# A hybrid decoder layer in fp32: transposed rows kept as two halves in DRAM, one root for four tiles of q and k, and the engine of low halves and sums set by stage

## The chip, the cores and the metric

The kernel runs on one core of a Trainium2 chip. The metric is the device time of one execution in microseconds, and a kernel is judged by the median of several executions. Engines are named as the profile names them: PE does matrix products (PEld loads their weights), DVE is the vector engine, ACT the scalar engine, POOL is GpSimd, and SP issues all DMA transfers. Each engine works through its own list of instructions strictly in order.

## The reference, cut to what matters

One decoder layer on 2048 tokens of width 1024. A projection feeds two groups of heads, a short convolution and a dilated attention; their outputs are projected back, and a gated feed-forward layer and a gated embedding follow.

```python
h = rmsnorm(x, g_mix);  zb, zc, zx, zq, zk, zv = split(h @ w_in)          # 6 x 512 columns
y_c = zb * causal_dwconv3(zc * zx, conv_w, conv_b)
q = rmsnorm(zq by head of 64, q_norm_g);  k = rmsnorm(zk by head of 64, k_norm_g)
y_a = dilated_attention(q, k, zv)          # three causal windows, ALiBi, merged by denominators
x = x + concat(rmsnorm(y_c, g_out_conv), rmsnorm(y_a, g_out_attn)) @ w_out
h = rmsnorm(x, g_ffn)
x = x + (silu(causal_dwconv3(h @ w_gate)) * (h @ w_up)) @ w_down           # d_ff = 2816
x = x + sigmoid(rmsnorm(x, g_ple) @ w_ple_gate) * (p @ w_ple_proj)
```

## The kernel before, in words

**Products.** Every fp32 operand is split into a high half (`split`: a cast on ACT) and a low half (source minus high half, L94, on DVE or POOL), and `mm3` (L97) sums three products: high by high, high by low, low by high. Transposes go through PE (L124, L198, L799).

**Stages.** By the trace: `qkv` runs from 0 to about 345 us, `mix` (attention, with the convolution's products woven in) to about 980, then `rest`: `project` to about 1200, `gate_up(0)` to 1660, `down(0)` to 1875, `gate_up(1)` to 2310, `down(1)` to 2530, `ple` to the end. Four blocks c of 512 tokens, each of four tiles j of 128, are worked through in `qkv`.

**qkv.** `head` normalizes a tile of x (root on one column, L75 to L84, then `hn`, L115), transposes it and splits it into `hT` (halves, L126 and L127). POOL then adds the two halves again (L173, 128x1024) into a staging tile `raw` and SP stores that fp32 sum to `hd[c]`. The staging tiles are three, and `load_w` loads the weights through the same three. `project` multiplies, and `normed` (L187 to L190) takes a tile of q or k in PSUM: squares on ACT, sums per head and a root of 8 columns on DVE, then the scaled tile `qn` or `kn`, read from PSUM. A root is 12 small instructions (`rsqrt`: three of set-up, then three rounds of three). `spill` transposes q or k once all four tiles are there and stores them to `qd` or `kd`, from where the attention loads `qs` and `kk`.

**The convolution's rows.** `load_conv_h(c)` loads `hd[c]` again, eight tiles of 128x512, and splits each into `hq`: a cast on ACT, a subtraction on POOL. It runs for c = 0 before the attention begins, and once for each further c in the midst of it.

**rest.** `stream` loads weights and splits them into operands `w`, up to four ahead of the products. The engine of the low half is `shared()`: a turn through three, of which one goes to POOL and two to DVE. `shared()` also places the sums of squares in `project` (`square`, L830) and a sum in `down` (L1048). A generator in the background prepares the other operand of the next stage (`right`): seven low halves for each quarter, of which those of indices 4 and 6 are named DVE and those of 5 and 3 POOL. `products` and `left` are one level of Strassen's scheme, hence seven products where there were eight. `reciprocal_root` makes a column of sums by PE (L836), copies it to SBUF (L838), takes a root on DVE (12 small instructions, L840 at its end), and the four evacuations of the product (L902) wait for it. `sums_of_w_down` makes, during `gate_up(0)`, four differences of each pair of rows of w_down (L959, 128x512, DVE) for the later stage.

**The order.** A scheduler places the instructions on each engine when the program is built; the source order is a preference and no guarantee.

## Time and profile before

| what | value |
|---|---|
| median of 3 executions | 2756.98 us (2752.61 to 2761.0) |
| the profiled execution, its own time | 2758.95 us |
| its span, first to last instruction | 2757.2 us |
| mean granted TensorE clock | 0.983 |
| busy: PE, DVE, ACT, POOL | 2621.5, 2006.8, 1321.2, 784.3 us |

Busy time of an engine counts an instruction from its start to its end, including time in which it was held up inside. Time idle before an instruction is put down to what released it. The clock of PE has two levels, 1.2 and 2.4 GHz, and the profile gives the granted share of the higher one.

### The profile page before, as it was taken

To read this page: it belongs to the slowest core of one execution; us is meant where nothing else is said; L and a number is where in the kernel's file an instruction comes from. 1 tells how busy PE (TensorE), PEld (TensorE's weight loads), DVE (VectorE), ACT (ScalarE), POOL (GpSimd) and SP (SyncE) were. 2 spreads that over 40 slices of the span, in tenths; PEclk is the share of its full clock that TensorE was granted. 3 is DMA by queue.
4 is the path that set the end of the run, shared out by engine and by line. 5 is a ranking of instruction groups with operands and counts; after the bars stand their busy time and mean duration, and the time that the engine had idled before them with its cause. 6 is when DMAs were issued, how large, how long until landed. Compare 5 with 4: busy or idle time off the path is not lost. (4 is left out here: it accounts for less than half of the span.)

```text
span 2757.2 us, 37506 instructions
## 1 busy us (share of the span) xinstructions
PE 2621.5 (95%) x12320; PEld 2169.0 (79%) x12320; DVE 2006.8 (73%) x3878; ACT 1321.2 (48%) x2941; POOL 784.3 (28%) x527
## 2 busy tenths in 40 slices
PE   7999989999999989899999999989999999998999
PEld 5777878888888778777788888767888887877887
DVE  8766656867677665998888778567888877557655
ACT  3332357877777344454344345444444435444332
POOL 5111311524343621123222223122222223223332
PEclk9999989999999999999999999999999999999999
DMA  5544565665756688568633346663323336666332
GB/s 191 153 138 123 169 163 139 184 184 146 205 154 180 220 279 296 196 228 274 241 114 105 107 142 227 216 233 115 102 101 107 104 111 218 220 217 204 103 130 85
DMA packets 283860, 470.04 MB, mean 170 GB/s; under 512 B 32656, under 2 KB 101904, under 8 KB 283664
## 3 DMA queue, kind: packets, MB, share of 16 engines
q1 hardware_dynamic: 283664, 467.64, 53.4%
q8 instruction: 97, 1.59, 0.2%
q14 instruction: 99, 0.81, 0.1%
HBM read 339.53 MB, written 127.99 MB: 170 GB/s over the span
## 5 line engine op out<-in xcount | busy, mean ns | idle before, releaser
L97 PE MATMUL ps<-t,w 128*128 128x512 f32 x4368 | 1024.3, 395 | 16.1 <-DVE w L94 9.5
L97 PEld LDWEIGHTS ps<-t,w 128*128 128x128 f32 x4368 | 819.6, 188 | 207.7 <-DVE w L94 12.4
L97 PE MATMUL ps<-w,g 128*128 128x512 f32 x1368 | 339.0, 397 | 26.9 <-DVE t L902 6.2
L97 PEld LDWEIGHTS ps<-w,g 128*128 128x128 f32 x1368 | 257.3, 190 | 89.0 <-DVE t L902 7.3
L94 POOL TENSOR_TENSOR w<-raw,w 128x512 fp32r<-128x512 f32 x100 | 144.9, 1449 | 564.1 <-ACT w L93 364.0
L97 PE MATMUL zps<-hq,chi 128*128 128x512 f32 x768 | 256.8, 411 | 5.3 <-DVE yc L327 5.3
L93 ACT CAST w<-raw 128x512 fp32r<-128x512 f32 x318 | 193.7, 616 | 119.5 <-PE ps L97 111.7
L289 POOL TENSOR_TENSOR clo<-craw,chi 128x512 fp32r<-128x512 f32 x96 | 126.4, 1322 | 389.8 <-ACT chi L288 144.2
L93 ACT CAST w<-s 128x512 fp32r<-128x512 f32 x208 | 128.3, 619 | 224.7 <-PE ps L97 200.5
L97 PE MATMUL ps<-w,t 128*128 128x512 f32 x852 | 211.6, 394 | 9.1 <-DVE w L94 5.9
L94 POOL TENSOR_TENSOR w<-s,w 128x512 fp32r<-128x512 f32 x70 | 111.8, 1597 | 368.7 <-ACT w L93 300.0
L438 ACT ACTIVATE pt<-so,md 128x256 f32<-128x256 f32 (+1 forms) x384 | 175.1, 458 | 79.9 <-DVE md L435 78.0
L97 PEld LDWEIGHTS ps<-w,t 128*128 128x128 f32 x852 | 159.0, 188 | 49.5 <-DVE w L94 8.8
L94 DVE TENSOR_TENSOR w<-raw,w 128x512 fp32r<-128x512 f32 x218 | 177.1, 816 | 15.5 <-ACT w L93 15.5
L435 DVE CUSTOM_DVE_ANT_0 so<-s,neg 128x256 f32<-128x256 f32 (+1 forms) x384 | 130.4, 362 | 60.9 <-PE s L432 47.3
L97 PEld LDWEIGHTS zps<-hq,chi 128*128 128x128 f32 x768 | 142.3, 195 | 29.6 <-DVE yc L327 6.1
L97 PE MATMUL zps<-hq,clo 128*128 128x512 f32 x384 | 154.3, 402 | 0.0
L432 PE MATMUL s<-kk,qs 128*128 128x256 f32 (+1 forms) x384 | 136.8, 360 | 11.8 <-DMA kk<-kd 9.1
L431 PE MATMUL s<-kk,qs 128*128 128x256 f32 (+1 forms) x384 | 132.8, 352 | 14.7 <-DMA kk<-kd 12.2
L471 DVE TENSOR_TENSOR nb<-po,nb 64x512 f32<-64x512 f32 x96 | 92.2, 961 | 65.0 <-ACT nb L470 64.2
L94 DVE TENSOR_TENSOR g<-g 128x512 fp32r<-128x512 f32 x84 | 72.6, 867 | 88.5 <-ACT g L93 88.5
L453 DVE TENSOR_TENSOR plo<-ptp,phi 128x512 fp32r<-128x512 f32 (+1 forms) x160 | 103.6, 653 | 30.9 <-ACT phi L452 30.2
(221 smaller groups left out, 4917.4 us busy)
## 6 DMA issues: line engine op xcount, KB each, us to landing
gd<-t SPq DMA_DIRECT2D x110, 256.0 KB, 2.0
craw<-in_w_conv_dram SPq DMA_DIRECT2D x96, 256.0 KB, 4.0
raw<-in_w_gate_dram SPq DMA_DIRECT2D x44, 512.0 KB, 3.8
raw<-in_w_up_dram SPq DMA_DIRECT2D x44, 512.0 KB, 3.7
g<-gd SPq DMA_DIRECT2D x84, 256.0 KB, 5.1
raw<-td SPq DMA_DIRECT2D x40, 512.0 KB, 4.5
t<-gd SPq DMA_DIRECT2D x70, 256.0 KB, 4.6
v<-vd SPq DMA_DIRECT2D x264, 64.0 KB, 2.7
```

Of the source, the lines that this page charges most:

```text
L93: self.nc.scalar.copy(hi, src)
L94: lo_engine.tensor_tensor(lo, src, hi.bitcast(F32), ALU.subtract)
L97: mm = lambda *a, **k: self.nc.tensor.matmul(*a, **k, **kw)
L289: nc.gpsimd.tensor_tensor(lo, raw, hi.bitcast(F32), ALU.subtract)
L431: mm(s[:, lo:], qb[l], cols[0], start=True, stop=False)
L432: mm(s[:, lo:], qb[l], cols[1], start=False, stop=True)
L435: nc.vector.tensor_tensor_reduce(out=so[:, lo:], in0=s[:, lo:], in1=neg[:, br, lo:], scale=-slope, scalar=3.0e38, op0=ALU.add, op1=ALU.min ...
L438: nc.scalar.activation(pt[:, l, lo:], so[:, lo:], AF.Exp, bias=md[:, 0, col:col + 1], scale=-1.0, accum_out=md[:, 1, col:col + 1])
L453: nc.vector.tensor_tensor(lo[:, i:i + n], tp[:, :n], hi[:, i:i + n].bitcast(F32), ALU.subtract)
L471: nc.vector.tensor_tensor(dst, like(po[other], br), dst, ALU.add)
```

## The change

The change has three parts. **Halves:** `hd` holds both halves of the transposed rows; two DMAs store them straight from `hT`, and one DMA of twice the size loads a tile of `hq`. The sum on POOL, the cast on ACT and the subtraction on POOL are gone. **Roots:** `squares` takes the squares on ACT, copies the product from PSUM to SBUF on ACT and sums per head on DVE; `normed` takes one root of 32 columns for four tiles and scales the four SBUF tiles in place, q after the last projection by k, k after the projections by v. **Engines:** `shared()` turns through `cycle`, which is 1 in `project` (all on POOL), 2 in `down` (half and half), else 3; in `right` the four fixed low halves become `shared()`; two of the four differences of w_down go to POOL.

```diff
-        self.hd = [d.tile([KD, P, QT], F32, name=f"hd{c}") for c in range(NQ)]
+        self.hd = [d.tile([KD, P, 2, QT], F32, name=f"hd{c}") for c in range(NQ)]
...
-        self.turn = (self.turn + 1) % 3
+        self.turn = (self.turn + 1) % self.cycle
         return self.nc.vector if self.turn else self.nc.gpsimd
...
-                t = stage.tile([P, KD, P], F32, name="raw", tag="raw")
-                nc.gpsimd.tensor_tensor(t, hT[:, :, 0].bitcast(F32), hT[:, :, 1].bitcast(F32), ALU.add)
-                nc.sync.dma_start(self.hd[c][:, :, j * P:(j + 1) * P].rearrange("k p n -> p k n"), t)
+                for s in range(2):
+                    nc.sync.dma_start(self.hd[c][:, :, s, j * P:(j + 1) * P].rearrange("k p n -> p k n"), hT[:, :, s].bitcast(F32))
...
-            def normed(ps, dst):
+            def squares(ps, dst, ss):
                 sq = work.tile([P, NH, HD], F32, name="sq", tag="sq", bufs=1)
-                ss = work.tile([P, NH], F32, name="ss8", tag="ss8")
-                psv = ps.rearrange("p (h d) -> p h d", d=HD)
-                nc.scalar.activation(sq, psv, AF.Square)
+                nc.scalar.activation(sq, ps.rearrange("p (h d) -> p h d", d=HD), AF.Square)
+                nc.scalar.copy(dst, ps)
                 nc.vector.tensor_reduce(ss, sq, AX.X, ALU.add)
-                r = self.rsqrt(work, ss, NH, 1.0 / HD)
-                nc.vector.tensor_tensor(
-                    dst.rearrange("p (h d) -> p h d", d=HD), psv,
-                    r.unsqueeze(2).broadcast_to([P, NH, HD]), ALU.mult)
+            def normed(tiles, ss):
+                r = self.rsqrt(work, ss.rearrange("p j h -> p (j h)"), 4 * NH, 1.0 / HD)
+                for j, t in enumerate(tiles):
+                    t = t.rearrange("p (h d) -> p h d", d=HD)
+                    nc.vector.tensor_tensor(
+                        t, t, r[:, NH * j:NH * j + NH].unsqueeze(2).broadcast_to([P, NH, HD]), ALU.mult)
...
-            raw = t[:, 1].bitcast(F32)
-            self.nc.sync.dma_start(raw, self.hd[c][k])
-            self.split(t[:, 0], t[:, 1], raw, self.nc.gpsimd)
+            self.nc.sync.dma_start(t.bitcast(F32), self.hd[c][k])
...
-                put(4, t1, nc.vector)
+                put(4, t1, self.shared())
...
-                put(5, t2, nc.gpsimd)
+                put(5, t2, self.shared())
...
-                minus = lambda t, x, y: nc.vector.tensor_tensor(t, x, y, ALU.subtract)
+                minus = lambda t, x, y: (nc.vector if t is b21 or t is b22 else nc.gpsimd).tensor_tensor(t, x, y, ALU.subtract)
...
             for name, *arg in stages:
+                self.cycle = dict(project=1, down=2).get(name, 3)
```

In the built program 99 instructions of 128x512 move from DVE to POOL: 54 of L94 for streamed weights, 16 sums of squares, 7 low halves net in the prepared operands and in `ple`, and 22 differences of w_down. POOL loses 16 sums of 128x1024 and 32 subtractions of 128x512. ACT loses 32 casts and gains 32 copies. The order of PE is nearly the same, stage by stage.

POOL at the start of `qkv`; `w0l` to `w2l` are low halves of the weights, `raw<-hT` the sum. Before:

```order
L94 TENSOR_TENSOR w0l<-raw,w0h 128x1024
L173 TENSOR_TENSOR raw<-hT 128x1024
L94 TENSOR_TENSOR w1l<-raw,w1h 128x1024 x2
...
L94 TENSOR_TENSOR w2l<-raw,w2h 128x1024 x4
L173 TENSOR_TENSOR raw<-hT 128x1024 x12
L289 TENSOR_TENSOR clo<-craw,chi 128x512 x2
L94 TENSOR_TENSOR hq<-hq 128x512 x8
```

POOL at the same place in the changed kernel, up to the convolution's weights (`clo`):

```order
L95 TENSOR_TENSOR w0l<-raw,w0h 128x1024 x2
L95 TENSOR_TENSOR w1l<-raw,w1h 128x1024 x4
L95 TENSOR_TENSOR w2l<-raw,w2h 128x1024 x4
L294 TENSOR_TENSOR clo<-craw,chi 128x512 x32
L541 TENSOR_TENSOR ya<-nb_2945,wb 128x512
```

The sums between the weights' low halves are gone, so that these stand in one row ahead of the convolution's.

DVE after the first tile's sums per head (L188) in `qkv`; `rs_` are a root's steps, 128x8 for q, 128x1 for the next tile of x. Before:

```order
L188 TENSOR_REDUCE ss_268<-sq 128x8
L75 TENSOR_SCALAR rs_h<-ss_268 128x8
L75 TENSOR_SCALAR rs_h<-ss 128x1
L76 TENSOR_SCALAR rs_i<-rs_h 128x8
L76 TENSOR_SCALAR rs_i<-rs_h 128x1
L77 TENSOR_SCALAR rs_y<-rs_i 128x8
L77 TENSOR_SCALAR rs_y<-rs_i 128x1
L82 TENSOR_TENSOR rs_u<-rs_y 128x8
L80 SCALAR_TENSOR_TENSOR rs_u<-rs_y,rs_h 128x1
```

DVE at the same place in the changed kernel:

```order
L188 TENSOR_REDUCE ssh<-sq 128x8
L76 TENSOR_SCALAR rs_h<-ss 128x1
L77 TENSOR_SCALAR rs_i<-rs_h 128x1
L78 TENSOR_SCALAR rs_y<-rs_i 128x1
L81 SCALAR_TENSOR_TENSOR rs_u<-rs_y,rs_h 128x1
L128 TENSOR_TENSOR hT<-tp,hT 128x4x128
L85 SCALAR_TENSOR_TENSOR rs_y<-rs_u,rs_y 128x1
```

The root of q no longer alternates with the root of the next tile; only the latter is left there.

POOL in `project`, behind the last sum of the attention's merge (`ya`); `u` are sums of squares, `w` low halves of w_out, `t` prepared operands. Before:

```order
L540 TENSOR_TENSOR ya<-ya,yt 128x512
L830 TENSOR_TENSOR u<-u,e 128x512
L94 TENSOR_TENSOR w<-raw,w 128x512 x2
L830 TENSOR_TENSOR u<-u,e 128x512 x2
L94 TENSOR_TENSOR w<-raw,w 128x512
...
L94 TENSOR_TENSOR w<-raw,w 128x512 x3
L94 TENSOR_TENSOR t<-e,t 128x4x128 x2
```

POOL there in the changed kernel:

```order
L545 TENSOR_TENSOR ya<-ya,yt 128x512
L835 TENSOR_TENSOR u<-u,e 128x512 x3
L95 TENSOR_TENSOR w<-raw,w 128x512 x4
L835 TENSOR_TENSOR u<-u,e 128x512 x6
L95 TENSOR_TENSOR w<-raw,w 128x512 x3
...
L835 TENSOR_TENSOR u<-u,e 128x512 x4
...
L95 TENSOR_TENSOR w<-raw,w 128x512 x8
L95 TENSOR_TENSOR t<-e,t 128x4x128 x4
```

The same kinds of instruction follow each other, two to three times as many, in longer runs.

## Rows read from the trace of the kernel before

**Rows 1.** Busy time by stage: PE, PEld, DVE, ACT, POOL (count), PEclk, DMA share, GB/s

```profile
0.00:345.00 345.00, 320.33 (x1472) 256.94 (x1473) 256.12 (x725) 111.18 (x188) 86.16 (x49) 1.00 0.50 155
345.00:890.00 545.00, 507.67 (x2983) 460.08 (x2982) 380.00 (x1152) 392.39 (x1106) 187.70 (x145) 0.96 0.63 168
890.00:980.00 90.00, 79.21 (x346) 64.33 (x345) 57.18 (x78) 34.10 (x62) 53.88 (x40) 0.94 0.64 210
980.00:1200.00 220.00, 204.46 (x928) 165.55 (x927) 167.88 (x330) 108.41 (x211) 36.87 (x26) 0.98 0.76 256
1200.00:1660.00 460.00, 448.23 (x1953) 362.82 (x1952) 383.10 (x550) 198.89 (x418) 120.84 (x75) 0.99 0.51 173
1660.00:1875.00 215.00, 203.63 (x870) 163.30 (x869) 134.71 (x191) 104.64 (x202) 52.98 (x36) 0.98 0.66 221
```

**Rows 2.** What PE waited for: us in total, times, longest us

```profile
PE ps L97 <- DVE w L94: 18.7, 15, 4.0
...
PE ps L97 <- DVE hT L127: 8.6, 5, 3.8
...
PE zps L97 <- DVE yc L327: 5.3, 2, 4.1
```

**Rows 3.** Timeline of the start: start us, duration us, instruction, [idle before <- releaser]

```profile
16.27 2.42 POOL L173 TENSOR_TENSOR raw<-hT 128x1024 f32<-128x1024 f32 x1 [3.47 <-DVE hT L127]
...
16.91 4.13 DVE L80 SCALAR_TENSOR_TENSOR rs_u<-rs_y,rs_h 128x1 f32<-128x1 f32 x2
...
23.51 1.07 PE L124 MATMUL tp<-ident,hn 128*128 128x128 f32 x8 [2.79 <-DVE hn L115]
...
37.84 2.46 POOL L173 TENSOR_TENSOR raw<-hT 128x1024 f32<-128x1024 f32 x1
...
42.60 2.37 DVE L80 SCALAR_TENSOR_TENSOR rs_u<-rs_y,rs_h 128x1 f32<-128x1 f32 x1
...
46.60 1.22 PE L97 MATMUL ps<-w0h,hT 128*128 128x512 f32 x2 [3.81 <-DVE hT L127]
...
52.44 0.63 PE L97 MATMUL ps<-w0h,hT 128*128 128x512 f32 x2
```

**Rows 4.** Groups of DVE and of POOL, 0 to 345 us: count, busy us, mean ns

```profile
L77 DVE TENSOR_SCALAR rs_y<-rs_i 128x8 int32<-128x8 int32 x32 | 28.9, 902 | 0.6
...
L173 POOL TENSOR_TENSOR raw<-hT 128x1024 f32<-128x1024 f32 x16 | 39.2, 2450 | 198.1 <-DVE rs_h L75 179.7 <-issue 9.7 <-DVE hT L127 8.6
```

**Rows 5.** Durations by line: ns minimum/median/maximum, first and last start

```profile
L77 DVE TENSOR_SCALAR rs_y<-rs_i x62: 139/172/2308, 6.1 to 2546.7; 128x8 int32<-128x8 int32 x34, 128x1 int32<-128x1 int32 x16, 128x4 int32<-128x4 int32 x12
...
L94 DVE TENSOR_TENSOR w<-raw,w x218: 615/684/1789, 920.2 to 2520.2; 128x512 fp32r<-128x512 f32 x109
...
L94 POOL TENSOR_TENSOR w<-raw,w x100: 1268/1297/2957, 923.1 to 2515.0; 128x512 fp32r<-128x512 f32 x100
...
L753 DVE TENSOR_TENSOR u<-ps,u x104: 674/684/692, 1201.0 to 2740.2; 128x512 f32<-128x512 f32 x104
...
L93 ACT CAST hq<-hq x32: 602/622/673, 307.6 to 896.6; 128x512 fp32r<-128x512 f32 x32
...
L759 ACT COPY u<-ps x52: 567/580/590, 1197.6 to 2729.7; 128x512 f32<-128x512 f32 x52
```

**Rows 6.** Timeline of the convolution's tail

```profile
923.57 1.75 DVE L257 SCALAR_TENSOR_TENSOR tap<-ext,cw,tap 128x512 f32<-128x512 f32 x1
...
927.50 1.22 PE L97 MATMUL zps<-hq,chi 128*128 128x512 f32 x2 [4.10 <-DVE yc L327]
```

**Rows 7.** Timeline of a root in `project`

```profile
1008.09 1.24 DVE L83 TENSOR_TENSOR rs_u<-rs_u,rs_h 128x4 f32<-128x4 f32 x1
...
1014.42 2.05 PE L97 MATMUL ps<-w,g 128*128 128x512 f32 x6 [3.21 <-DVE t L902]
```

**Rows 8.** A stretch of 5 us while the convolution's rows load, columns as in Rows 1

```profile
315.00:320.00 5.00, 5.00 (x23) 4.03 (x22) 4.83 (x8) 0.48 (x2) 3.00 (x3) 1.00 0.24 65
```

**Rows 9.** Timeline of PE where the attention begins

```profile
354.78 0.48 PE L431 MATMUL s<-kk,qs 128*128 128x128 f32 x1 [5.00 <-DMA kk<-kd]
```

More of the change, by code (lines that the diff above doesn't have):

```diff
@@ L46, in __init__ @@
         self.turn = 0
+        self.cycle = 1
         self.const = ctx.enter_context(tc.tile_pool(reuse_waits="tile", name="const", bufs=1))
@@ L215, in qkv @@
                 hTs = []
+                sq, sk = [work.tile([P, 4, NH], F32, name="ssh", tag="ssh", bufs=4) for _ in range(2)]
                 qn = [work.tile([P, 512], F32, name="qn", tag=f"qn{j}", bufs=1) for j in range(4)]
@@ L219, in qkv @@
                     hTs.append(head(c, j, load_x(c, j) if c or j else first))
-                    normed(project(hTs[j], 0), qn[j])
+                    squares(project(hTs[j], 0), qn[j], sq[:, j])
                     if c == 0 and j == 1:
@@ L226, in qkv @@
                 for j in range(4):
-                    normed(project(hTs[j], 1), kn[j])
+                    squares(project(hTs[j], 1), kn[j], sk[:, j])
                 if c == NQ - 1:
@@ L230, in qkv @@
                     self.open_conv()
+                normed(qn, sq)
                 spill(c, qn, self.qd, gq)
@@ L239, in qkv @@
                                       vt.rearrange("p q s d -> p (q s d)").bitcast(F32))
+                normed(kn, sk)
                 spill(c, kn, self.kd, gk)
@@ L731, in right @@
                 minus(t2, b22, t1)
-                put(6, t3, nc.vector)
+                put(6, t3, self.shared())
                 yield
@@ L736, in right @@
                 minus(t4, b21, t2)
-                put(5, t2, nc.gpsimd)
+                put(5, t2, self.shared())
                 yield
-                put(3, t4, nc.gpsimd)
+                put(3, t4, self.shared())
                 yield
```

## The prediction

> **What bounds the kernel now.** I read first the busy time by stage [rows 1]. PE is the engine to shorten: in gate_up(0) it is busy 448.23 of 460 us, in qkv 320.33 of 345, and a product that is never held up has nothing to gain from this change, which takes no work from PE. So the most there is to win is PE's idle time, 2757.2 - 2621.5 = 135.7 us, and what the clock loses behind idle stretches. By stage that is 24.7 us in qkv, 37.3 in the attention, 10.8 in the convolution's tail, 15.5 in project, 11.8 in gate_up(0) and 11.4 in down(0). The second view is what PE waited for [rows 2]: low halves of weights by DVE 18.7 us, low halves of the transposed rows 8.6, the convolution's last product 5.3. So DVE, late by a little, ends most of what the change can touch. The third view shows why DVE is late. It is busy 383.10 of 460 us in gate_up(0), but part of that is being held up. The same subtraction takes 684 ns in the middle and up to 1789; on POOL it takes 1297 [rows 5]. An addition with one operand in PSUM never exceeds 692 [rows 5]. In qkv a step of a root on 128x8, one of 32, takes 902 ns on average [rows 4], although such a step takes 172 in the middle [rows 5]; two steps took 4.13 us beside POOL's sum of 2.42 and what follows it [rows 3]. So an instruction of DVE that reads SBUF waits until POOL's running instruction ends, about 1.1 us for 128x512 (1789 - 684).
>
> **qkv, the sums and the roots.** POOL loses 16 sums of 2450 ns [rows 4], 39.2 us. DVE loses 24 roots of 12 steps. None of this lies on PE's path by itself; what counts is the idle time that DVE causes. Two gaps at the start come from it: 2.79 us at 23.51 and 3.81 us at 46.60 [rows 3]. In the first, DVE's two steps are held by two POOL instructions in turn, the sum and then a weight's low half; the sum goes, the low half remains and moves forward, so I take half of 4.13, 2.1 us. In the second a sum of 2.46 us heads a row of POOL work, so that is the gain. The order shows that nothing else takes its place on POOL. Together 4.5 us, between nothing (the weights' low halves, earlier now, hold DVE just as long) and 6.6. Behind the second gap two products take 1.22 us where later ones take 0.63 [rows 3], the lower of PE's two clocks, granted after the idle time; I add 1 us, between 0 and 2. **Term: -5.5, bounds 0 and -8.6.** The rest is hidden. 32 copies from PSUM on ACT at 580 ns [rows 5] are 18.6 us, beside 111 us busy in 345, and they free a PSUM bank before the root is made. The roots for four tiles stand one group of products ahead of the transposes that need them: for q some 27 products of v stand between the first and the second pair of transposes, and 80 products by k ahead of them.
>
> **The doubled rows.** hd is stored as two DMAs instead of one and loaded in tiles of 512 KB. Each store waits for DVE's `hT` instead of POOL's sum behind it, so SP's queue, with the next x behind it, is free earlier. The load ahead of the attention is 2.1 MB more. At 256 GB/s with a DMA share of 0.76 [rows 1] the full rate is 337, so it costs 6.2 us of all DMA engines. In the 5 us after the load they stand at 0.24 [rows 8], 3.8 us free. What is left, 2.4 us at most, could push `kd` and lengthen the 5.00 us that PE waits for `kk` [rows 9]. **Term: +1, bounds 0 and +2.4.** The three later loads fall in the attention, where DMA is at 0.63 and ACT busy 392 of 545 us [rows 1]. ACT loses 24 of the 32 casts of 622 ns there [rows 5], 15 us; POOL loses as many subtractions. PE waits there mostly on loads and on the attention's own chain, so **term: -1, bounds -4 and +4** (a load of `kk` behind a doubled `hq` in SP's order).
>
> **The convolution's tail.** PE waits 4.10 us for `yc` [rows 6]. Ahead of it DVE does low halves of w_out, and its own filter step is held, 1.75 us [rows 6]. In the change those low halves go to POOL and the subtractions of the last `hq` leave it. DVE loses three of 684 ns, POOL holds others back: I take 2 us of the gap and 1 for the clock, granted at 0.94 in this stretch [rows 1]. From above the cost is three low halves of 1297 ns [rows 5] ahead of the convolution's own on POOL, 3.9 us; from below the whole gap. **Term: -3, bounds -4.1 and +3.9.**
>
> **project.** All streamed low halves, sums of squares and four low halves of each prepared quarter go to POOL: 26 instructions in the stage become some 65 in the order. The chain that PE waits for is on DVE: a root in small steps with other work between them, then four evacuations. The order shows about two low halves fewer between a root's first and last step, 1.4 us; against it every step can meet POOL's instruction, 1.24 us instead of 0.2 [rows 5, 7]. The 3.21 us there [rows 7] is the size of one such chain's delay. **Term: -2, bounds -8 (half the idle time) and the slower rival below.**
>
> **gate_up and down.** 22 differences go to POOL, and 33 low halves in the two downs. DVE saves 684 ns for each and is held 1.1 us where the next instruction reads SBUF; which of these happens I put at about even, so nothing is left. **Term: 0, bounds -6 and +6.**
>
> **Sum.** -5.5 + 1 - 1 - 3 - 2 + 0 = -10.5. The profiled execution took 2758.95 us (span 2757.2 and 1.75 around it), so 2748.5 on its terms. It lies 2.0 above the median of the runs, 2756.98, so 2746.5 for the median; I say **2747**, and the bounds, which need not fall together (root of the squared distances, project's upper one at 8), give 2737 to 2761.
>
> **The rivals.** *The lock eats it.* 99 instructions of 128x512 move to POOL. They save 99 x 0.684 = 68 us of DVE and cost up to 99 x 1.1 = 109 us of waiting in it. If most of them meet an instruction that reads SBUF, DVE ends with some 40 us more, spread over stages where it is busy 63 to 83%. PE idle of a tenth of that, 4 us, and no gain in the tail or in project leave -5.5 + 1 + 4, about **2756**. For it: every stage behind the attention has DVE instructions near 1.7 us. Against it: evacuations and other instructions that read PSUM are not held [rows 5], and POOL loses 80 us in qkv and mix (39.2, and 32 subtractions at about 1.3). The Trainium skill states it as a rule, in "SBUF — State Buffer", section "SBUF: two separate sides": the port pair that VectorE and GpSimd share is an exclusive lock for a whole instruction, taken by a VectorE instruction with two SBUF inputs. By it the scaling of q and k, which now reads two SBUF operands, can be held too. The trace agrees for the subtraction (684 to 1789) and for the one with a PSUM operand (692 at most).
>
> *Slower: the roots in project.* There are eight roots, each of 12 steps on one queue. POOL's runs are now three to eight long, and each of its instructions lets about one step of DVE pass. If three more steps of each are held for 1.04 us (1.24 - 0.2), eight chains end 25 us later, and PE, with four PSUM banks waiting for the evacuations, stands for it. -5.5 - 3 + 25 + 3 (the clock) gives **2776**. It decides once a root ends later than the products that follow it; two streamed operands take 24 products, 5.6 us at 0.234 us each (870 in 203.63 us) [rows 1], and the chain of 3.21 us of idle time shows that the margin is already used up. Against it: DVE has less work between the steps.
>
> *Faster: all waits for DVE's halves go.* The 18.7 us for streamed weights and 8.6 us for `hT` [rows 2] end, with the clock's loss: **2729**.
>
> *The doubled transfers decide.* Each of the four loads puts 2.4 us on PE, which eats the gain in qkv: **2760**. It is the case in which the change moves work to DMA and does not free PE.
>
> **How the numbers follow.** A measurement tells a change from none from about 0.3%, 8.3 us. The forecast has 0.46 (0.30 of it under 2748.7, for its sum lies just below that bound), the lock 0.18, all waits gone 0.18, the slow roots 0.13, the transfers 0.05. Faster by over 0.3%: 0.30 + 0.18 = 0.48; within: 0.16 + 0.18 + 0.05 = 0.39; slower: 0.13. The range reaches from 2728, the faster rival, to 2765, above the lock and the transfers; it leaves out the slow roots and some edges.
>
> **What would show it.** POOL in qkv falls from 86 us to about 37, DVE from 256 to under 180, and both early gaps shrink; if the gaps stay, the first term was wrong, and the weights' low halves alone hold DVE. The wait for `yc` under 2.5 us shows the tail right. In project POOL rises to about 85 us; waits of PE on L902 and its successor above 10 us in all, or steps of a root in rows of 1.2 us, show the slow rival. DVE in gate_up(0) within 10 us of 383 shows the exchange even. The wait for `kk` at the attention's start above 7 us shows the transfers. The forecast is wrong if PE's idle time in the stages behind 980 us changes by more than what qkv gives.

## The result, and the profile after

The changed kernel took 2789.74 us (median of 4 executions, 2785.81 to 2790.0) where before took 2758.99 (2752.61 to 2765.1) beside it. The ratio is 1.0112, 95% interval 1.0094 to 1.0129, so it is about 31 us slower. I had said 2747 and 2728 to 2765. The profiled execution took 2790.0 us (span 2788.2, mean granted clock 0.980; before 0.983).

Busy time by stage of the changed kernel follows, columns as in [rows 1]. The borders are those of [rows 1], moved so that each stage holds nearly the same products (1484 in qkv where [rows 1] have 1472), and I add down(1).

```profile
0.00:340.00 340.00, 321.21 (x1484) 258.64 (x1485) 186.24 (x440) 123.06 (x212) 38.92 (x27) 1.00 0.61 192
340.00:896.00 556.00, 507.34 (x2990) 459.17 (x2988) 382.50 (x1153) 386.32 (x1097) 164.16 (x126) 0.96 0.64 173
896.00:987.00 91.00, 77.22 (x329) 61.13 (x328) 48.93 (x66) 27.09 (x46) 55.51 (x41) 0.93 0.68 219
987.00:1212.00 225.00, 211.33 (x935) 170.56 (x935) 168.68 (x290) 107.99 (x211) 96.76 (x67) 0.95 0.74 250
1212.00:1679.00 467.00, 447.90 (x1945) 360.98 (x1944) 379.69 (x524) 198.07 (x416) 147.79 (x96) 0.99 0.50 167
1679.00:1901.00 222.00, 206.67 (x873) 164.92 (x873) 136.09 (x181) 105.79 (x204) 80.05 (x51) 0.98 0.64 218
...
2336.00:2560.00 224.00, 206.64 (x874) 163.97 (x872) 143.43 (x170) 102.92 (x198) 78.96 (x51) 0.98 0.65 219
```

qkv moved as forecast: POOL 38.92 us there instead of 86.16 [rows 1], DVE 186.24 instead of 256.12, and the stage is 5 us shorter at these round borders, 7.8 by the count below. Every later stage that is shown is longer, though DVE's busy time in them changes by 8 us at most. What PE waited for (us in total, times, longest) shows where:

```profile
PE s L437 <- DMA v<-vd: 23.9, 6, 5.6
PE ps L98 <- POOL w L95: 17.2, 13, 5.1
PE ps L98 <- DVE w L95: 13.8, 14, 3.5
...
PE ps L98 <- DVE g L830: 9.3, 5, 3.3
PE s L436 <- DMA kk<-kd: 7.1, 4, 4.0
...
PE zps L98 <- DVE yc L332: 5.1, 2, 4.9
PE ps L98 <- DVE hT L128: 4.8, 4, 1.4
```

The same rows before, so far as [rows 2] do not have them:

```profile
PE s L431 <- DMA kk<-kd: 12.2, 5, 5.0
...
PE s L432 <- DMA kk<-kd: 9.1, 5, 4.0
...
PE ps L97 <- POOL w L94: 5.7, 7, 2.2
...
PE s L432 <- DMA v<-vd: 2.6, 2, 1.7
```

Waits for DVE's streamed halves fell from 18.7 to 13.8 us and those for `hT` from 8.6 to 4.8. Waits for POOL's streamed halves rose from 5.7 to 17.2. The waits put down to `v` rose from 2.6 to 23.9, but the products that wait there read `kk` and `qs`, and the waits put down to `kk` fell. Loads of both together make 31.0 us, where before they made 23.9.

PE executes 12,320 instructions in both programs. The scheduler put 351 of the 1484 in qkv and 1725 of the 2916 in the attention in another place, but each of these stages holds the same instructions as before, so the start of the n-th at a stage's border can be compared. The table gives how much longer each stage is than in the profiled execution of before (us; a stage ends where the 1484th, 4400th, 4784th, 5648th, 7600th, 8480th, 10344th and 11240th starts), for the changed kernel and for the experiments. In the last column stands the ratio of the timed executions with its interval.

| kernel | qkv | attention | tail | project | gate_up(0) | down(0) | gate_up(1) | down(1) | ple | ratio |
|---|---|---|---|---|---|---|---|---|---|---|
| changed | -7.8 | +9.7 | +4.2 | +5.9 | +7.0 | +6.5 | -0.1 | +1.9 | +3.8 | 1.0112 (1.0094 to 1.0129) |
| halves | -5.5 | +13.6 | +1.3 | +0.5 | +1.8 | +0.3 | -0.5 | -0.5 | -1.7 | 1.0000 (0.9986 to 1.0014) |
| roots | -4.2 | +2.2 | -0.7 | -0.6 | -0.6 | -1.2 | +2.0 | -0.3 | -0.8 | 0.9987 (0.9974 to 0.9999) |
| halves_roots | -8.1 | +15.0 | -0.2 | +0.6 | +2.9 | -2.9 | -0.5 | -1.2 | +1.0 | 1.0006 (0.9993 to 1.0020) |
| engines | +1.0 | -2.3 | -0.4 | +5.7 | +2.5 | +6.8 | +1.0 | +6.8 | +3.7 | 1.0072 (1.0053 to 1.0090) |
| proj_pool | -1.5 | +8.6 | +0.5 | +4.2 | -1.0 | -6.6 | +2.4 | -9.8 | +6.2 | 0.9982 (0.9968 to 0.9997) |
| down_half | -0.6 | +0.7 | -1.1 | -0.7 | +0.7 | -2.8 | +2.7 | -5.2 | +5.7 | 1.0011 (0.9996 to 1.0025) |
| right_turn | -0.9 | +1.9 | -0.5 | -0.8 | +2.4 | -3.0 | -0.1 | -9.2 | +2.2 | 0.9976 (0.9959 to 0.9993) |
| minus_pool | -0.3 | +1.6 | -1.3 | +1.9 | +4.8 | -0.8 | +0.5 | -3.2 | -0.9 | 1.0010 (0.9995 to 1.0024) |
| right_down | +0.4 | +1.0 | -1.3 | -1.1 | +4.7 | +8.1 | +0.6 | +2.9 | +6.1 | 1.0066 (1.0046 to 1.0086) |
| right_down_own | +0.3 | +2.8 | -1.3 | -2.4 | -2.8 | -2.0 | +2.1 | -5.2 | +5.4 | 1.0001 (0.9991 to 1.0012) |
| one_back | -1.1 | +4.6 | +2.1 | -1.8 | +3.3 | +4.3 | +0.4 | +2.6 | +5.3 | 1.0059 (1.0037 to 1.0081) |
| after_right_fixed | -6.7 | +10.1 | +4.2 | +6.4 | +0.9 | -4.8 | -0.5 | -1.9 | +1.1 | 1.0036 (1.0023 to 1.0049) |
| phase | -0.4 | +1.1 | -1.8 | -0.4 | +0.4 | -6.0 | +0.2 | -7.8 | +4.7 | 0.9960 (0.9946 to 0.9974) |
| phase2 | -1.4 | +4.8 | -1.3 | -0.7 | +1.2 | -2.9 | +0.3 | +1.3 | +1.5 | 1.0023 (1.0013 to 1.0034) |
| regular | +0.1 | +4.3 | -0.6 | -1.8 | -1.2 | -1.6 | +0.3 | -3.5 | +1.8 | 0.9978 (0.9963 to 0.9993) |
| phase_roots | -1.9 | +2.8 | -1.3 | +0.3 | -0.1 | -7.1 | +0.5 | -8.2 | +5.3 | 0.9963 (0.9950 to 0.9976) |
| raw_act_roots | +1.7 | +4.7 | -0.4 | +0.3 | -0.4 | -2.7 | +0.1 | -4.3 | +0.9 | 1.0005 (0.9993 to 1.0018) |
| hq_double | -0.5 | +15.6 | -0.5 | +0.1 | +0.7 | -3.4 | -0.5 | -0.3 | +1.7 | 1.0029 (1.0016 to 1.0042) |

A stage of one profiled execution is no exact number: the attention is 8.6 us longer in proj_pool and down(1) 4.3 shorter in raw_act_roots, where the code of these stages is untouched. The profiled executions of halves and of proj_pool lie 7.6 and 5.9 us above the median of their twelve, so that their columns overstate a loss. Five kernels that leave the downs as they were (halves, roots, halves_roots, raw_act_roots, hq_double) lie at -3.4 to +0.3 in down(0) and -4.3 to -0.3 in down(1), so that only what goes beyond this counts there. So I read a column by groups of kernels, and let the timed ratios decide.

### The profile page after: what moved, and what is told of

Same layout as the page of the kernel before. It is cut to its first block, busy times and chain, and to the rows that moved or that the text cites. A ratio compares the mean times of both kernels' runs of the same rounds, so it can differ in the third digit from the quotient of the medians.

```text
span 2788.2 us, 37155 instructions
## 1 busy us (share of the span) xinstructions
PE 2632.2 (94%) x12320; PEld 2172.1 (78%) x12320; DVE 1938.0 (70%) x3491; ACT 1318.7 (47%) x2941; POOL 852.5 (31%) x578
## 4 chain that ended last, share of the span: by engine, by line
PE 41%; DMA 8%; issue 7%; DVE 7%; POOL 3%; ACT 1%; SPq 1%; DVEq 0%; POOLq 0%; ACTq 0%
PE ps L98 40%; DMA g<-gd 2%; POOL w L95 2%; DMA g<-in_w_down_dram 1%; DVE w L95 1%; DVE t L95 1%; DMA u<-in_w_ple_gate_dram 1%; PE tp L804 1%; PE tp L98 1%; DVE u L727 0%; DVE g L830 0%; DVE s L707 0%; DMA g<-xd 0%; DMA craw<-in_w_conv_dram 0%; DMA wb<-wd 0%
## 5 line engine op out<-in xcount | busy, mean ns | idle before, releaser
L95 POOL TENSOR_TENSOR w<-raw,w 128x512 fp32r<-128x512 f32 x154 | 227.3, 1479 | 482.5 <-ACT w L94 391.9
L98 PE MATMUL ps<-w,g 128*128 128x512 f32 x1368 | 345.1, 402 | 27.6 <-DVE g L830 9.3
L98 PEld LDWEIGHTS ps<-w,g 128*128 128x128 f32 x1368 | 261.3, 193 | 91.7 <-DVE g L830 11.8
L94 ACT CAST w<-raw 128x512 fp32r<-128x512 f32 x318 | 193.3, 616 | 107.8 <-PE ps L98 97.2
L94 ACT CAST w<-s 128x512 fp32r<-128x512 f32 x208 | 128.2, 619 | 229.3 <-PE ps L98 208.7
L437 PE MATMUL s<-kk,qs 128*128 128x256 f32 (+1 forms) x384 | 137.4, 361 | 28.6 <-DMA v<-vd 23.9
L95 DVE TENSOR_TENSOR w<-raw,w 128x512 fp32r<-128x512 f32 x164 | 141.7, 866 | 3.6 <-ACT w L94 2.5
L437 PEld LDWEIGHTS s<-kk,qs 128*128 128x128 f32 x384 | 107.0, 279 | 32.3 <-DMA kk<-kd 10.4
L95 DVE TENSOR_TENSOR w<-s,w 128x512 fp32r<-128x512 f32 x138 | 111.4, 808 | 23.0 <-ACT w L94 22.9
```

The source lines that it names most:

```text
L94: self.nc.scalar.copy(hi, src)
L95: lo_engine.tensor_tensor(lo, src, hi.bitcast(F32), ALU.subtract)
L98: mm = lambda *a, **k: self.nc.tensor.matmul(*a, **k, **kw)
L437: mm(s[:, lo:], qb[l], cols[1], start=False, stop=True)
```

## Experiment 1: the three parts apart

Three kernels have one part of the change each, a fourth has halves and roots together; the diff is the one shown above, cut to the part.

> Before, with the halves part alone (hd in two halves, no sum on POOL, no cast and subtraction for hq). Before is 2759 us. Theory A (the engine choice makes the whole loss; the two other parts act as predicted, about -8 in qkv and little elsewhere): 2752 to 2759, attention no longer than before. Theory B (the doubled rows cost the attention, since a load of 512 KB stands ahead of v and kk in SP's order): qkv 3 to 6 us shorter, attention with the tail 8 to 12 us longer, 2762 to 2768, waits of PE on v above 15 us instead of 2.6. Theory C (each part only reshuffles the order that the scheduler builds, and the stages move by a few us in both directions): any value from 2750 to 2770, with changes of more than 3 us in gate_up and down, where the code is untouched.

> Before, with the roots part alone (ACT copies q and k to SBUF, one root for four tiles). Before is 2759 us. Theory A and B: qkv 0 to 4 us shorter, the attention and the rest as before, 2755 to 2760; the idle gap of 3.81 us in the first 50 us shrinks by under 2 us, since POOL's sum is still there, and DVE's busy time in qkv falls by about 50 us. Theory C: the stages behind 980 us move by more than 3 us though their code is untouched.

> Before, with the engine choice alone (turn of 1 in project, 2 in down, 3 elsewhere; the four prepared low halves by turn; two differences of w_down on POOL). Before is 2759 us. Theory A: project +6, gate_up(0) +7, down(0) +7, down(1) +3, ple +3, so about +26, 2785. Theory B: about +26 less what a late start of project explains, 2773 to 2780, and the attention as before. Theory C: under +12, 2765 to 2771, with the loss in other stages than in the changed kernel.

> Before, with halves and roots, so the changed kernel with the engine choice taken back. Before is 2759 us, the changed kernel 2790. Theory A: qkv 8 us shorter, the attention and the tail as before, 2749 to 2753. Theory B: qkv 8 us shorter, the attention and the tail 10 to 14 us longer, 2761 to 2766. Theory C: a value that is not the sum of the two parts alone, by more than 8 us.

Measured: halves 2760.63 us, roots 2755.55, engines 2781.73, halves and roots 2763.4, before 2759.09 beside them. The engine choice alone makes 0.72% of the 1.12%: theory A in its main point. But the kernels halves and halves_roots do not keep the 5.5 and 8.1 us that they win in qkv, since the attention is 13.6 and 15.0 us longer: theory B there, though halves, with 2760.63 us, lies below the 2762 that it said. Theory C is not needed for these four: no column moves by more than 3 us in a stage whose code or loads they leave alone. One expectation for roots failed: the gap of 3.81 us [rows 3] was to shrink by under 2 us, since POOL's sum is still there, and it is 0.53 us.

```profile
43.48 0.73 PE L97 MATMUL ps<-w0h,hT 128*128 128x512 f32 x2 [0.53 <-DVE hT L127]
```

## Experiment 2: the four pieces of the engine choice

```diff
# proj_pool
+                self.cycle = dict(project=1).get(name, 3)
# down_half
+                self.cycle = dict(down=2).get(name, 3)
# right_turn: likewise t3, t2 and t4
-                put(4, t1, nc.vector)
+                put(4, t1, self.shared())
# minus_pool
-                minus = lambda t, x, y: nc.vector.tensor_tensor(t, x, y, ALU.subtract)
+                minus = lambda t, x, y: (nc.vector if t is b21 or t is b22 else nc.gpsimd).tensor_tensor(t, x, y, ALU.subtract)
```

> Before, with all of the low halves and sums of squares that are placed by turn in project on POOL (turn of 1 there, 3 elsewhere); 37 instructions move. Before is 2759 us, all engine choices together took 2782, +20 by the ratio. Theory L (what costs is a low half that PE waits for and that POOL brings later, in stages that stream weights): +5, 2764, with the loss in project and nothing behind it. Theory K (every instruction on POOL holds up DVE, and the loss goes by the number of instructions moved, 20 us for 99 of them, 0.2 us each): +7.5, 2766.5, the loss in project too. Not separated by this run alone.

> Before, with every second low half and sum of down on POOL instead of every third (turn of 2 in down); 33 low halves of w move. Before is 2759 us. Theory L: down(0) +6 and down(1) +6, 2770 to 2773, waits of PE on POOL's low halves above 8 us in the two stages where they were 3.5. Theory K: 33 x 0.2 = 6.6, 2764 to 2767, spread over waits for DVE.

> Before, with the four low halves of a prepared quarter placed by turn (two fixed on DVE and two fixed on POOL before); 7 instructions move net, to POOL. Before is 2759 us. Theory L: these are prepared a stage ahead and nobody waits for them, so 0 to +2, except that they shift which streamed half falls on POOL: 2757 to 2763. Theory K: 7 x 0.2 = 1.4, 2760.

> Before, with two of the four differences of each pair of rows of w_down on POOL; 22 instructions move, all in gate_up(0). Before is 2759 us. Theory L: nobody on PE waits for a difference, but POOL's streamed low halves stand behind them: 0 to +2.5, 2759 to 2761.5, one wait of PE on POOL's low half near 5 us in gate_up(0). Theory K: 22 x 0.2 = 4.4, 2763.5, spread over several waits for DVE.

Measured: ratios 0.9982, 1.0011, 0.9976 and 1.0010. They add up to -0.21%, and together the four made +0.72%. Theory L falls with down_half, which was to be 6 us longer in each down and is shorter in both. Theory K falls with proj_pool, which was to lose 7.5 us and lost none; the intervals of down_half and minus_pool alone would still allow its 6.6 and 4.4 us. right_turn tests neither, for its turn moved eight instructions the other way: POOL executes 519 there, 527 in before, where the expectation had 7 more. And proj_pool is 6.6 and 9.8 us shorter in the two downs, which it doesn't touch, except that the turn stands elsewhere when they begin. That gave the next theory, P: not how many low halves fall on POOL, but which, one after the other.

## Experiment 3: which streamed halves, not how many

```diff
# phase
+                self.turn = dict(gate_up=2, down=1, ple=2).get(name, self.turn)
# right_down: right_turn and down_half together
# right_down_own: the same, but the prepared halves have a counter of their own
+    def apart(self):
+        self.own = (self.own + 1) % self.cycle
+        return self.nc.vector if self.own else self.nc.gpsimd
...
+                put(4, t1, self.apart())
```

> Before, with one line added: the turn is set to 1 ahead of each down (it stood at 0 there in before) and to 2 ahead of gate_up and ple, where it stood already. The number of instructions on each engine stays the same to one or two; another of each three streamed low halves goes to POOL. proj_pool showed down(0) 6.6 and down(1) 9.8 us shorter though it left down's code alone; only the turn's state differed there. Theory P (which of the streamed low halves fall to POOL decides, more than how many): down(0) and down(1) 6 to 10 us shorter each, 2742 to 2750. Theory L or K (the number on POOL decides): within 3 us of 2758. Theory C (any rebuild moves stages by several us at random): any value, with changes in gate_up or ple as large as in down.

> Before, with the four prepared low halves placed by turn and a turn of 2 in down. Alone the two gave 0.9976 and 1.0011 of before. If the parts add: 0.9987, 2755. Theory P: with the prepared halves drawing from the same turn, the streamed halves no longer alternate but come in pairs on POOL (in the run of all engine choices POOL took 2 in a row 8 times in down(0)), so down(0) and down(1) are 5 to 8 us longer each, 2768 to 2775.

> As right_down (four prepared low halves by turn, a turn of 2 in down), but the prepared halves draw from a counter of their own, so that the streamed halves alternate strictly; as many instructions fall on POOL as in right_down, to one or two. right_down took 1.0066 of before. Theory P (the interleaving, hence two streamed halves in a row on POOL, makes the loss): 0.998 to 1.002, 2754 to 2765, and no streamed half on POOL of 6.5 us at the end of down(0). If the number on POOL decides after all: 1.005 or more, 2773 and up.

Measured: phase 2749.47 us, 0.9960. Its list of PE's instructions is that of before row for row, and down(0) and down(1) are 6.0 and 7.8 us shorter. right_down 2780.23 us, 1.0066, where its two parts alone would add up to 0.9987; that is even above theory P's 2768 to 2775. right_down_own 2757.81 us, 1.0001, and the loss is gone. POOL executes 554 instructions in right_down, 552 in right_down_own and 555 in down_half (1.0011), so their number doesn't make it. What differs is that the prepared halves draw from the streamed halves' counter. The streamed halves of down(0), in the order in which they start (worked out from the traces; P on POOL, a dot on DVE):

```
before          .P..P..P..P..P..P..P..P.P...P..P..P..P..P..P..P....P..P..P....P..P.P.....
changed         P..P.PP..PP.P.P..P.P..P..PP...P.P.PP.P.PP.PP.P.P..PP...PP..PP..P.P.PP.P.PP
right_down      P..P.P.P.PP.P.P..P.P..P..PP...P.P.PP.P.PP.PP.P.P..PP...PP..PP..P.P.PP.P.P
right_down_own  .P..P.P.P.PP..P.P.P.P.PP..P.P.P.P.P.P.P.P.P.P.P.P.PP..P.P.P.P.P.P.P.P.P.P
phase           .P..P.P..P.P...P..P..P..P..P..P..P.P...P..P..P..P.P.P...P..P.P..P..P..P.P
```

With a turn of 2, a prepared half that draws in between shifts the alternation: pairs on POOL, then pairs on DVE. right_down has nine pairs on POOL here, right_down_own three, with 36 halves on POOL in both. In phase, POOL has 108 halves `w<-raw,w` in the whole program where before has 100 [rows 5], and six sums `s<-s,e` fewer; so two things change, which halves and how many. Experiment 4 sets them apart. PE's waits for streamed halves (all stages) are 11.8 us for DVE where [rows 2] have 18.7:

```profile
PE ps L97 <- DVE w L94: 11.8, 13, 4.4
PE ps L97 <- POOL w L94: 9.0, 7, 2.7
```

By stage, waits for DVE's halves fell from 3.9 to 0.6 us in down(0) and from 5.3 to 0.8 in down(1), and those for POOL's rose from 3.5 to 6.2 in the two together. Its two downs run at the full clock throughout, with fewer than 9 us of idle time of PE each (PE 200.91 of 209 us; before 0.98 and 203.63 of 215):

```profile
1659.00:1868.00 209.00, 200.91 (x870) 161.87 (x869) 135.09 (x189) 104.54 (x202) 56.94 (x37) 1.00 0.67 225
2301.00:2514.00 213.00, 204.02 (x885) 164.14 (x883) 140.56 (x182) 103.19 (x194) 65.72 (x39) 1.00 0.69 232
```

The waits of right_down beside those of right_down_own:

```profile
PE ps L98 <- DVE w L95: 26.4, 21, 2.7
...
PE ps L98 <- POOL w L95: 11.1, 13, 4.8
```

```profile
PE ps L103 <- POOL w L100: 11.0, 11, 2.5
PE ps L103 <- DVE w L100: 9.5, 9, 3.6
```

Over the whole program, waits for POOL's halves are the same 11 us, and those for DVE's are 26.4 instead of 9.5. By stage it looks otherwise. In down(0), where right_down loses most, it is POOL's halves that come late, in right_down first, then in right_down_own:

```profile
PE ps L98 <- POOL w L95: 7.7, 6, 4.8
```

```profile
PE ps L103 <- POOL w L100: 2.4, 2, 1.3
```

Waits for DVE's halves are nearly equal there (2.9 and 2.1 us), and those for ACT's casts 4.1 and 0.8. Of the 26.4 us, 14.1 stand in gate_up(0), where right_down_own has 5.5. The scheduler also places SP's transfers otherwise in each of these kernels, in phase too, where PE's list is unchanged. So the runs show that with a turn of 2 the shared counter makes the loss; that pairs on POOL are the whole of how it does so is argued.

## Experiment 4: the third state, a regular row, and the changed kernel with one piece back

```diff
# phase2
+                self.turn = dict(gate_up=2, down=2, ple=2).get(name, self.turn)
# regular: a counter of three of its own for the streamed halves of project and down
-                        self.split(t[:, 0], t[:, 1], raw[0][:, i], self.shared())
+                        self.split(t[:, 0], t[:, 1], raw[0][:, i], self.apart())
# after_right_fixed: the changed kernel, without
-                put(4, t1, nc.vector)
+                put(4, t1, self.shared())
# phase_roots: phase and roots
```

> Before with the turn set to 2 ahead of each down, the third of its three states (0 is before's, 1 gave 0.996). Theory P: a time of its own in down(0) and down(1), by which streamed halves fall on POOL, from 8 us shorter to 8 us longer, all other stages within 3 us of before. If state 1 was faster only because before's pattern has stretches without POOL: down(0) and down(1) near those of state 1, 0.996 to 0.998.

> Before, with one edit: the streamed low halves of project and down draw from a counter of their own, again of three, so that exactly each third of them goes to POOL, undisturbed by sums and by other stages. The number on POOL changes by a few. Theory P: a regular row is as good as the best state of the turn seen here (0.996), 0.995 to 0.999. If only the particular halves of state 1 matter: anything from 0.996 to 1.003, by where the row of three begins.

> The changed kernel with the four prepared low halves put back to their fixed engines (one on DVE, one on DVE, two on POOL); all else as changed. The changed kernel took 1.0112 of before. Theory P: the loss of right and down together goes, what is left is halves and roots (1.0006) and the small parts (0.9982, 1.0011, 1.0010): 1.001 to 1.003, 2761 to 2768. If the loss of the changed kernel has a further cause in the engine choice: 1.006 or more, 2776 and up.

> Before with the turn set to 1 ahead of each down (0.996 alone) and with the roots part (0.9987 alone). If they add: 0.9947, 2745, the best of all kernels here. If the shorter qkv is eaten in the attention as with the halves: 0.996, 2748.

Measured: phase2 2764.43 us, 1.0023; regular 2753.58, 0.9978. So the three states of the turn ahead of down give 1, 0.9960 and 1.0023, which is 17 us between the best and the worst. These two have 529 instructions on POOL each, and 108 and 107 of the halves `w<-raw,w` among them, so the number of POOL's halves doesn't make the difference; which halves they are does, with the order of transfers that the scheduler builds for them. The profiled execution of phase2 doesn't show where it loses: its downs are 2.9 shorter and 1.3 us longer. A regular row is better than before by its interval; whether it is as good as state 1 is open, since their intervals overlap. after_right_fixed took 2767.91 us, 1.0036: one piece of four instructions a quarter taken back returns 0.76% of the 1.12%, where gate_up(0) goes from +7.0 to +0.9 and down(0) from +6.5 to -4.8. That lies a little above what the parts let me expect (1.001 to 1.003). The column of the tail (+4.2) has one reason, that of project another: the four kernels that have project's halves on POOL are 4.2 to 6.4 us longer there, the fifteen others -2.4 to +1.9. proj_pool had hidden this behind what its turn won in the downs. phase_roots took 2746.75 us, 0.9963, no better than phase alone: the gain of the roots shows no sign of adding, and the intervals don't settle it. phase and phase_roots are both faster than before and than the changed kernel by their intervals.

## Experiment 5: one instruction

In the changed kernel, in engines and in right_down one and the same streamed half takes 6.52 us on POOL near the end of down(0), where the median was 1.30 [rows 5]. The timeline of the changed kernel, POOL first, then DVE, then PE (start us, duration us, instruction, [idle before <- releaser]):

```profile
1847.33 6.52 POOL L95 TENSOR_TENSOR w<-raw,w 128x512 fp32r<-128x512 f32 x1 [3.59 <-issue]
1853.81 1.72 POOL L95 TENSOR_TENSOR t<-u,t 128x512 fp32r<-128x512 f32 x1
...
1846.62 1.88 DVE L95 TENSOR_TENSOR t<-u,t 128x512 fp32r<-128x512 f32 x3
1848.42 0.68 DVE L1053 TENSOR_TENSOR s<-s,e 128x512 f32<-128x512 f32 x1
1849.03 0.68 DVE L727 TENSOR_TENSOR u<-u 128x512 f32<-128x512 f32 x1
1849.63 0.68 DVE L95 TENSOR_TENSOR g<-g 128x512 fp32r<-128x512 f32 x1
1850.23 0.68 DVE L95 TENSOR_TENSOR w<-raw,w 128x512 fp32r<-128x512 f32 x1
1850.83 0.68 DVE L727 TENSOR_TENSOR u<-u 128x512 f32<-128x512 f32 x1
1851.43 0.68 DVE L95 TENSOR_TENSOR t<-t 128x512 fp32r<-128x512 f32 x1
1852.03 2.36 DVE L95 TENSOR_TENSOR g<-g 128x512 fp32r<-128x512 f32 x2
...
1853.90 2.50 PE L98 MATMUL ps<-w,g 128*128 128x512 f32 x5 [5.11 <-POOL w L95]
```

DVE's instructions follow each other every 0.6 us and take 0.68, so each has begun before the one ahead has ended. All go from SBUF to SBUF, and until POOL's begins none of them is held. POOL's instruction is, from 1847.33 on; it ends at 1853.85, so its own 1.3 us begin at about 1852.55, between the two subtractions of `g`, the second of which is held in turn (2.36 us for the two). PE stands for 5.11 us.

```diff
# one_back: right_down, with
+                        self.streamed += 1
+                        engine = self.shared()
+                        self.split(t[:, 0], t[:, 1], raw[0][:, i], nc.vector if self.streamed == 96 else engine)
```

> As right_down, with one single instruction moved: the streamed low half that takes 6.52 us on POOL near the end of down(0) goes to DVE, where such a one takes 0.68. right_down took 1.0066 of before, 2780. If that one instruction, held up while DVE goes through a row of instructions without a pause, makes PE's wait of 5 us and the low clock behind it: down(0) 5 to 8 us shorter than in right_down, 1.004 to 1.005, 2770 to 2775. If POOL's queue is late anyway, another wait takes its place: within 2 us of right_down, 2778 to 2782.

Measured: 2775.54 us, 1.0059 (1.0037 to 1.0081), against 1.0066 of right_down; the intervals lie over each other, so by the time alone it is open. The traces tell more. In right_down, then in one_back:

```profile
1833.52 6.52 POOL L95 TENSOR_TENSOR w<-raw,w 128x512 fp32r<-128x512 f32 x1 [3.59 <-issue]
...
1840.09 2.50 PE L98 MATMUL ps<-w,g 128*128 128x512 f32 x5 [4.81 <-POOL w L95]
```

```profile
1838.63 4.63 POOL L96 TENSOR_TENSOR t<-u,t 128x512 fp32r<-128x512 f32 x1 [6.10 <-ACT t L95]
...
1829.29 1.45 PE L99 MATMUL ps<-w,g 128*128 128x512 f32 x5 [0.84 <-POOL w L96]
...
1838.56 1.49 PE L99 MATMUL ps<-w,g 128*128 128x512 f32 x4 [1.81 <-DVE g L96]
```

The wait of 4.81 us is gone, three of 0.84 to 1.81 come instead, and down(0) is 3.8 us shorter (8.1 to 4.3). POOL's next instruction is now the one held, 4.63 us, but it is a half prepared for the next stage, and PE does not wait for it there. By these two executions this instruction makes up to half of down(0)'s loss in right_down; by the timed ratio its share is not shown. The rest, and the 4.7 us in gate_up(0) and 6.1 in ple, are spread over short waits that I can't put down to single instructions.

A long hold need not cost anything. POOL's streamed half is held for 5.94 us in regular (0.9978), for 6.03 in down_half (1.0011) and for 6.66 in phase2 (1.0023), all in down(1). In the 20 to 30 us around them PE waits 0.9, 0 and 0.3 us for POOL's halves. A hold costs where PE needs that half next.

## Experiment 6: the doubled loads of the convolution's rows

```diff
# hq_double: before, with both halves of a tile loaded with the same rows
-            self.nc.sync.dma_start(raw, self.hd[c][k])
+            self.nc.sync.dma_start(t.bitcast(F32), self.hd[c][k].unsqueeze(1).broadcast_to([P, 2, QT]))
# raw_act_roots: roots, and ACT copies the transposes from PSUM, in place of POOL's sum; hd stays single
+            if raw is not None:
+                nc.scalar.copy(raw[:, sl], tp)
```

> Before, with the load of each tile of hq doubled to 512 KB (the same rows twice; one half is overwritten by the cast as before). Casts and subtractions stay. Theory B1 (the bytes of the doubled loads delay v and kk): the attention 8 to 14 us longer, 2766 to 2772. Theory B2 (not the bytes; without the casts and subtractions the scheduler puts SP's transfers in another order): under 3 us, 2757 to 2762.

> Before, with the roots part, and with the fp32 rows for hd copied by ACT from the transposes' PSUM tiles instead of added on POOL; hd stays single, and the attention's code and transfers are those of before. Theory B (what the halves part loses is lost by its loads in the attention): qkv 7 to 9 us shorter as with halves and roots, the attention as before, 2749 to 2753. If the attention is 8 us or more longer here too, the loss comes from the order that the shorter qkv leaves behind, not from the loads.

Measured: hq_double 2768.24 us, 1.0029 (1.0016 to 1.0042), so 8 us for this edit. In the table the five kernels with doubled loads are 9.7 to 15.6 us longer in the attention (mean 12.8), the fourteen others -2.3 to +8.6 (mean 2.8). PE's waits in hq_double:

```profile
PE s L432 <- DMA v<-vd: 20.4, 6, 4.4
...
PE s L431 <- DMA kk<-kd: 8.4, 4, 3.3
```

SP's own timeline shows how. Behind the loads of `hq` for the second block stand 15 loads of `v`. The row is first from before, then from the changed kernel, then from hq_double; with the two latter goes what SP's queue waited for in the 25 us around it.

```profile
508.84 9.40 SPq L413 DMA_DIRECT2D v<-vd  x15
```

```profile
503.22 12.40 SPq L418 DMA_DIRECT2D v<-vd  x15
...
SPq L418 <- DMA hq<-hd: 5.5, 5, 1.4
```

```profile
511.19 12.78 SPq L413 DMA_DIRECT2D v<-vd  x15
...
SPq L413 <- DMA hq<-hd: 5.0, 5, 1.8
```

SP issues a `v` only when a tile of `hq` has landed, five times, and loses 3.0 and 3.4 us of issue time, with all that is queued behind: `wb`, then `kk` and `v` of the next heads. Before, no such wait stands there; over the whole attention SP waits for `hq` 2.9 us before, 11.0 in the changed kernel and 11.3 in hq_double. In the changed kernel the last `kk` of the next heads is issued at 556.5 us (557.5 before), while PE, ahead through qkv, is there 6 us earlier; it arrives and stands for 5.57 us, where before it stood for 1.72:

```profile
564.84 0.58 PE L437 MATMUL s<-kk,qs 128*128 128x256 f32 x1 [5.57 <-DMA v<-vd]
```

So theory B1's forecast came out, and doubling the loads costs 8 us by the timed ratio: what PE won in qkv it waits off at the loads. That the bytes alone do it is not shown. In the traces 1682 to 1725 of PE's 2916 instructions in the attention stand at another place than before in the five kernels with doubled loads, and none in the fourteen others, so the order that the scheduler then builds is a rival that no run sets apart. raw_act_roots, 1.0005, was to keep qkv's gain without doubled loads. Its attention is 4.7 us longer, like other kernels without them, but qkv gained nothing: DVE's low half of `hT` waits for ACT, which has two more copies to make, and PE waits for it at the start.

```profile
39.29 1.22 PE L97 MATMUL ps<-w0h,hT 128*128 128x512 f32 x2 [5.88 <-DVE hT L129]
```

So whether a shorter qkv lasts to the end with single loads was not settled by it; roots alone (-4.2 in qkv, 0.9987) suggests that most does, and phase_roots, no faster than phase, does not confirm it.

## Why the prediction was wrong, step by step

**qkv: right in the number, in part by luck.** The term was -5.5, measured -7.8, within its bounds. Of the two gaps the second, 3.81 us, is gone. I had put it down to POOL's sum, but it shrinks to 0.53 us in roots, where the sum still runs. The first stayed:

```profile
23.56 1.07 PE L125 MATMUL tp<-ident,hn 128*128 128x128 f32 x8 [3.11 <-DVE hn L116]
```

So the part of 2.1 us that I took for it was wrong, and the roots, which I had as hidden, gave -4.2 alone. DVE is busy 186.24 us in qkv, not under 180.

**The doubled rows in the attention: wrong in size.** The term was -1, bounds -4 and +4, and the load ahead of the attention +1. I counted bytes against free DMA time only at the start, and for the three later loads weighed a saving on ACT, which PE did not wait for. Measured is +9.7. The rival with 2.4 us on each of four loads, 9.6 us, had nearly the price (8 us in hq_double), and I gave it 0.05. It was not at the attention's start, where PE's wait for `kk` fell from 5.00 to 4.02 us. The step that failed was to price the loads by a stage's mean DMA share, 0.63, and to look only at `kk` behind them: the trace shows the delay in the queue of SP, in which loads of `v` stand behind `hq` and wait until its tiles have landed.

**The tail: wrong.** -3 was forecast, +4.2 measured; the wait for `yc` that should fall below 2.5 us is 4.89. Neither halves (+1.3) nor engines (-0.4) alone shows it, after_right_fixed (+4.2) does. The trace of the changed kernel has a second wait, of 4.29 us, which before does not have. DVE first, then PE:

```profile
960.46 1.63 DVE L545 TENSOR_TENSOR ya<-ya,yt 128x512 f32<-128x512 f32 x1
...
962.35 0.68 DVE L326 TENSOR_TENSOR ext<-zps,zc 128x512 f32<-128x512 f32 x1
...
963.08 1.22 PE L98 MATMUL zps<-hq,chi 128*128 128x512 f32 x2 [4.29 <-DVE ext L326]
```

Four instructions of the attention's merge (`yt`, `ya`) stand ahead of the convolution's `ext`, and three of them take over 1.6 us each. Before, `ext` came ahead of three of the four (at 953.78 us), and PE did not wait for it. after_right_fixed has the same wait, 4.27 us. So the order on DVE makes it; why the scheduler chose it there is open.

**project: wrong, and not by the rival I named.** -2 was forecast, +5.9 measured. The steps of a root did not slow down (L83 of before, L84 after: 296 ns on average before, 231 after), and waits for the evacuations are 2.9 us in all, so the slow roots fall. What is held instead is the low half of the other operand, `g`, which DVE makes just ahead of the products. The group in project, before and then after (count, busy us, mean ns, idle before):

```profile
L825 DVE SCALAR_TENSOR_TENSOR g<-s,go,g 128x512 fp32r<-128x512 f32 x44 | 33.8, 778 | 14.4 <-ACT g L824 14.3
```

```profile
L830 DVE SCALAR_TENSOR_TENSOR g<-s,go,g 128x512 fp32r<-128x512 f32 x44 | 49.6, 1137 | 20.4 <-ACT g L829 19.7 <-DMA s<-ycd 0.6
```

44 of them take 0.36 us more each, 15.8 us of DVE. In the three other kernels with project's halves on POOL the mean is 1006 to 1075 ns, in phase 754. PE waits 9.3 us for them in five waits (3.3 in four before), and the clock granted over the stage is 0.95 (0.98 before). I had looked for the chain that PE waited for in before, and not for the next one that POOL's lock could make late.

**gate_up and down: wrong, and the largest part.** The term was 0, bounds -6 and +6; measured is +15.3 in the two pairs of stages, and 3.8 more in ple, which I had left out. "Which of these happens I put at about even, so nothing is left" was the step that failed. The pieces alone, worth -0.24 to +0.11% each, do not contradict it. What I left out is that one turn serves three kinds of work, so that the change of four prepared halves changes which streamed halves go to POOL. The "7 low halves net" of the count hid a different sequence. Taking this piece back alone returned 0.76% (after_right_fixed). In gate_up(0) PE's waits for DVE's evacuations `u` (L758, L753 before) also rose, from 1.9 to 6.6 us, and minus_pool alone, with 4.1, has part of that.

**The lock was half seen.** I costed DVE's instruction that waits for POOL's one, 1.1 us. The other direction, POOL held by a row of DVE's instructions for 5 us, stood nowhere in the sum. The Trainium skill ("SBUF — State Buffer", section "SBUF: two separate sides") says that whichever starts first has the shared ports for its whole instruction and the other blocks. Read for one pair of instructions, that would have POOL wait for 0.68 us at most. The trace agrees for a single encounter (1.7 us for either engine's instruction), and shows a wait of about 5.2 us where DVE's instructions follow each other without a pause.

**What held.** Of the signs that I had named, POOL in qkv near 37 us (38.92) and DVE in gate_up(0) within 10 of 383 (379.69) came out as said, and POOL in project, 96.76, rose past the 85. PE still lost 7 us in gate_up(0): the busy time of DVE was the wrong thing to watch there. DVE in qkv, the first gap and the wait for `yc` did not come out. The last sign, idle time behind 980 us that changes by more than qkv gives, did, and by it the forecast is wrong.

## What to carry to other kernels

Where a counter deals work to two engines, list what each engine gets, one after the other, for every stage: two kinds of work that draw from one counter make a sequence that nobody chose, and here the state of the counter alone was worth 17 us at the same number of instructions on POOL. Test an engine choice with its pieces apart and in pairs, since pieces that cost nothing alone made 0.7% together. A saving on an engine that PE doesn't wait for was worth nothing here against doubled loads in a stage that waits for loads.

## What the runs showed of the hardware

An instruction of POOL on 128x512 that takes 1.3 us alone took 6.52 us behind a row of nine DVE instructions without a pause; DVE's own were not slowed meanwhile (0.68 us each). In the kernels regular, down_half and phase2 POOL's streamed half is held for 5.94, 6.03 and 6.66 us in down(1). So here POOL was shut out for many instructions of DVE and not for one, and the work that it was given to relieve DVE came latest where DVE was busiest.
